# PSUM in four tiles of two banks, and the whole first k tile on the sync queue, in a windowed matmul

## The chip, the cores and the metric

One core of a Trainium2 chip. The metric is device time in microseconds (us) of one execution; most executions agree within 0.3%. The span of a profile runs from its first to its last instruction and is about 1.8 us shorter than the time. TensorE is PE, VectorE is DVE, ScalarE is ACT, GpSimd is POOL and SyncE is SP in the profile.

## The reference

```python
# x [4, 4096, 4096] f32, w [4096, 4096] f32, offsets [4] int64
for b in range(4):
    o = int(offsets[b])
    out[b] = x[b, o:o+64] @ w          # out [4, 64, 4096] f32
```

All of w has to be read (67.1 MB), with 4 x 64 rows of x (4.2 MB), and 4.2 MB have to be written.

## The kernel before

The 256 rows are two groups g of 128. The rows of x are loaded, cast to fp16 and transposed by PE. w is streamed by the POOL queue in blocks of up to four k tiles (a k tile is 128 rows of w), cast to fp16 on the way, into three rotating buffers. Only k tile 0 comes as fp32 by two hardware queues, half of its columns on each, and is cast by ACT. PE writes its sums to tiles in PSUM. Each partial product of 512 columns fills one of eight tiles of 128x512 fp32, which the program names `bank0` to `bank7` and I call banks; it is then evacuated, that is read out and added to `acc` in SBUF, before the program has PE write to that bank again.

```python
ps = [psum_pool.tile([P, NT], fp32, name=f"bank{t}") for t in range(8)]      # NT = 512
...
nc.sync.dma_start(out=w0_32[:, :NG], in_=w[0:P, :NG])
nc.scalar.dma_start(out=off_t[:], in_=offsets[None, :])
nc.scalar.dma_start(out=w0_32[:, NG:], in_=w[0:P, NG:])
...
def add_out(bank, g, c):
    dst = acc[g][:, c * NT : (c + 1) * NT]
    nc.vector.tensor_add(out=dst, in0=dst, in1=ps[bank][:])

def whole_rows(kts, cols, first):          # a block of k tiles, bank after bank
    for g in range(G):
        for c in cols:
            bank = n_bank % 8; n_bank += 1
            for i, kt in enumerate(kts):
                mm(bank, g, kt, ...)
            add_out(bank, g, c)            # cut: the first block copies instead
...
def columns(ng, kts):                      # half of the columns, all 8 banks at once
    for ki in kts:
        for g in range(G):
            for j in range(n_sub):
                tail_mm(ki, g, ng, j, ki == kts[0], ki == kts[-1])
    for g in range(G):
        for j in range(0, n_sub, 2):       # even banks: VectorE adds, odd banks: ACT copies
            add_out(4 * g + j, g, ng * n_sub + j)
            nc.scalar.copy(out=tmp[2 * g + j // 2][:], in_=ps[4 * g + j + 1][:])
    for g in range(G):
        for j in range(1, n_sub, 2):       # then VectorE adds the copies
            nc.vector.tensor_add(...)

columns(order[1], list(join))              # k tiles 25 to 27, first half of the columns
columns(ng, list(join) + list(range(k_tail, n_k)))     # k tiles 25 to 31, second half
for g in range(G):
    store(nc.gpsimd, g, ng * NG, (ng + 1) * NG)        # 2 x 1 MB: the first stores
# cut: k tiles 28 to 31 of the first half, its adds, and four stores of 0.5 MB on two queues
```

I call the two calls of `columns` the short and the long accumulation.

## Time and profile before

| | before |
|---|---|
| time, median of 3 | 182.00 us (181.90 to 182.02) |
| span, mean granted clock | 180.2 us, 0.900 |
| PE / DVE / ACT busy | 127.2 / 90.6 / 18.3 us |
| HBM read / written | 71.30 / 4.19 MB |
| last wait of PE for w, at 164.42 | 0.77 us |
| first store issued | 166.15 us |

The page gives each engine's busy time and, in 40 slices, its busy share in tenths; a 9 is 90% or more. The chain of waits follows back what released what. A row of the timeline starts with start and length in us, and ends with how long the engine had been idle before it and what ended that. The prediction below shows these lines; here it is enough that the DMA engines are full from 3 us to about three before the end (share 0.98 from 3 to 5 us, 1.02 from 175 to 177.5).

### The profile page before, as it was taken

The numbers are of one execution on the slowest core, as the hardware profiler recorded it, in microseconds if no ns is written. First come the engines' busy times: TensorE is split into PE (matmuls) and PEld (weight loads), VectorE is DVE, ScalarE is ACT, GpSimd is POOL, SyncE is SP. The second block draws the span as 40 slices with busy tenths as digits, with TensorE's granted clock in tenths as the row PEclk, the third lists the DMA queues.
The fourth block names the chain that finished last, engine by engine and source line by source line (L and its number), as shares of the span: only waits on it lengthen the run. The fifth ranks groups of instructions, "written<-read, shape, count | busy, mean of one in ns | idle before, by whom it ended". The sixth has DMA issues, their size and how long they took to land.

```text
span 180.2 us, 1537 instructions
## 1 busy us (share of the span) xinstructions
PE 127.2 (71%) x576; PEld 57.0 (32%) x576; DVE 90.6 (50%) x136; ACT 18.3 (10%) x27; POOL 12.7 (7%) x27
## 2 busy tenths in 40 slices
PE   0000789104999499938996599949999999998900
PEld 0000754001344134403442134414444444443400
DVE  0000678100487347833686147725879966409560
ACT  2412556200000000000000000000000004004000
POOL 4600000000000100010001000020007100001100
PEclk9999999855699979996999569987999999999995
DMA  5999989999998899999989999989999999999995
GB/s 186 316 256 216 276 175 204 236 233 226 233 226 189 175 233 233 235 222 233 196 189 211 233 233 218 229 180 213 224 209 215 195 211 213 216 211 208 372 411 209
DMA packets 4152, 40.98 MB, mean 227 GB/s; under 512 B 434, under 2 KB 434, under 8 KB 2226
## 3 DMA queue, kind: packets, MB, share of 16 engines
q0 software_dynamic: 3280, 36.70, 93.4%
q1 hardware_dynamic: 432, 2.10, 3.2%
q10 hardware_dynamic: 434, 2.10, 2.9%
q8 instruction: 4, 0.07, 0.1%
q14 instruction: 2, 0.02, 0.0%
HBM read 71.30 MB, written 4.19 MB: 419 GB/s over the span
## 4 chain that ended last, share of the span: by engine, by line
DMA 58%; PE 30%; issue 3%; DVE 2%; another core or an unknown queue 1%; POOL 1%; POOLq 1%; DVEq 0%
DMA wc<-in_w_dram 58%; PE bank L150 30%; DVE acc L160 2%; POOL wc L114 1%; POOLq L71 1%; POOL xrow L78 0%; DVEq L259 0%; POOL identity masks.py:197 0%; POOLq L78 0%; POOL w L67 0%; POOLq masks.py:199 0%; POOLq L248 0%
## 5 line engine op out<-in xcount | busy, mean ns | idle before, releaser
L150 PE MATMUL bank<-wc,xT 128*128 128x512 f16 x480 | 115.0, 405 | 24.3 <-DMA wc<-in_w_dram 24.3
L160 DVE TENSOR_TENSOR acc<-acc,bank 128x512 f32<-128x512 f32 x112 | 75.2, 687 | 61.5 <-PE bank L150 60.9
L150 PEld LDWEIGHTS <-xT 128*128 128x128 f16 x512 | 52.1, 103 | 93.8 <-DMA wc<-in_w_dram 27.2
L136 PE MATMUL bank<-identity,xrow 128*128 128x128 f16 x64 | 5.3, 258 | 20.0 <-DMA xrow<-in_x_dram 20.0
L203 ACT COPY tmp<-bank 128x512 f32<-128x512 f32 x8 | 4.1, 599 | 127.5 <-PE bank L150 127.5
L145 DVE CAST xT<-bank 128x512 f16<-128x512 f32 x8 | 5.3, 687 | 21.0 <-PE bank L136 20.9
L95 POOL DMA_DIRECT2D wc<-in_w_dram x8 | 4.3, 540 | 108.1 <-PE bank L150 108.1
L136 PEld LDWEIGHTS <-xrow 128*128 128x128 f16 x64 | 5.0, 124 | 20.1 <-issue 20.1
L150 PE MATMUL bank<-w,xT 128*128 128x512 f16 x32 | 7.1, 379 | 0.0
L175 DVE COPY acc<-bank 128x512 f32<-128x512 f32 x8 | 5.4, 688 | 0.9 <-PE bank L150 0.6
L114 POOL DMA_DIRECT2D wc<-in_w_dram x6 | 3.9, 674 | 17.1 <-PE bank L150 17.1
L147 ACT CAST xT<-bank 128x512 f16<-128x512 f32 x8 | 4.4, 593 | 7.1 <-PE bank L136 7.0
L208 DVE TENSOR_TENSOR acc<-acc,tmp 128x512 f32<-128x512 f32 x8 | 5.0, 682 | 0.0
L177 ACT COPY acc<-bank 128x512 f32<-128x512 f32 x8 | 4.7, 586 | 2.1 <-PE bank L150 1.9
L193 POOL DMA_DIRECT2D out_dram<-acc x2 | 1.1, 538 | 26.6 <-DVE acc L208 26.6
L64 ACT CAST w<-acc 128x2048 f16<-128x2048 f32 x1 | 1.9, 1897 | 4.9 <-DMA acc<-in_w_dram 4.9
L78 POOL DMA_DIRECT2D xrow<-in_x_dram x4 | 2.1, 524 | 2.1 <-issue 2.1
L63 ACT CAST w<-acc 128x2048 f16<-128x2048 f32 x1 | 1.9, 1897 | 2.8 <-DMA acc<-in_w_dram 2.8
L63 ACT ACT_TABLE_LOAD x1 | 1.3, 1283 | 1.8 <-PEq L248 1.8
L67 POOL DMA_DIRECT2D w<-in_w_dram x1 | 0.7, 660 | 0.8 <-POOLq L248 0.8
masks.py:199 POOL TENSOR_SCALAR_AFFINE_SELECT identity<-identity 128x128 f16<-128x128 f16 x1 | 0.3, 290 | 0.1
masks.py:197 POOL MEMSET identity<- 128x128 f16 x1 | 0.2, 224 | 0.0
(4 smaller groups left out, 0.4 us busy)
## 6 DMA issues: line engine op xcount, KB each, us to landing
wc<-in_w_dram POOLq DMA_DIRECT2D x5, 4096.0 KB, 42.1
wc<-in_w_dram POOLq DMA_DIRECT2D x4, 1024.0 KB, 24.6
wc<-in_w_dram POOLq DMA_DIRECT2D x1, 3072.0 KB, 37.1
xrow<-in_x_dram POOLq DMA_DIRECT2D x4, 512.0 KB, 14.5
wc<-in_w_dram POOLq DMA_DIRECT2D x1, 2048.0 KB, 26.6
out_dram<-acc POOLq DMA_DIRECT2D x2, 1024.0 KB, 6.3
acc<-in_w_dram SPq DMA_DIRECT2D x1, 1024.0 KB, 5.1
w<-in_w_dram POOLq DMA_DIRECT2D x1, 1024.0 KB, 12.0
```

The lines of the kernel that those rows point to most:

```text
L63: nc.scalar.copy(out=w_one[0][:, :NG], in_=w0_32[:, :NG])
L95: nc.gpsimd.dma_start(out=t[:, base : base + r * N], in_=w[k0 * P : (k0 + r) * P, :].rearrange("(p r) n -> p (r n)", r=r),)
L114: nc.gpsimd.dma_start(out=t[:, pos : pos + n * wd].rearrange("p (t n) -> p t n", t=n), in_=w[ki * P : (ki + n) * P, ng * NG + c0 : ng * NG ...
L136: nc.tensor.matmul(out=ps[t][:, i * P : (i + 1) * P], lhsT=x_cols(g, 4 * t + i), rhs=identity[:], start=True, stop=True,)
L145: nc.vector.tensor_copy(out=dst, in_=ps[t][:])
L147: nc.scalar.copy(out=dst, in_=ps[t][:])
L150: nc.tensor.matmul(out=ps[bank][:], lhsT=xT[g][:, kt * P : (kt + 1) * P], rhs=rhs, start=start, stop=stop,)
L160: nc.vector.tensor_add(out=dst, in0=dst, in1=ps[bank][:])
L175: nc.vector.tensor_copy(out=acc[g][:, c * NT : (c + 1) * NT], in_=ps[bank][:])
L177: nc.scalar.copy(out=acc[g][:, c * NT : (c + 1) * NT], in_=ps[bank][:])
L203: nc.scalar.copy(out=tmp[2 * g + j // 2][:], in_=ps[4 * g + j + 1][:])
L208: nc.vector.tensor_add(out=dst, in0=dst, in1=tmp[2 * g + j // 2][:])
```

## The change

The intent: half as many evacuations, each over two banks, as one add of 1024 columns should take less than two of 512; and the scalar queue left to the offsets alone, which the loads of x wait for. The diff, cut:

```diff
-    tmp = [acc_pool.tile([P, NT], fp32, name=f"tmp{i}") for i in range(4)]
+    tmp = [acc_pool.tile([P, 2 * NT], fp32, name=f"tmp{i}") for i in range(G)]
-    ps = [psum_pool.tile([P, NT], fp32, name=f"bank{t}") for t in range(8)]
+    pairs = [psum_pool.tile([P, 2 * NT], fp32, name=f"banks{t}") for t in range(4)]
+
+    def banks(b, n=1):
+        return pairs[b // 2][:, b % 2 * NT : (b % 2 + n) * NT]
...
-    nc.scalar.dma_start(out=w0_32[:, NG:], in_=w[0:P, NG:])
+    nc.sync.dma_start(out=w0_32[:, NG:], in_=w[0:P, NG:])
...  (transposes and whole_rows: two banks filled, then one evacuation of 1024 columns)
-    def add_out(bank, g, c):
-        dst = acc[g][:, c * NT : (c + 1) * NT]
-        nc.vector.tensor_add(out=dst, in0=dst, in1=ps[bank][:])
+    def add_out(bank, n, g, c):
+        dst = acc[g][:, c * NT : (c + n) * NT]
+        nc.vector.tensor_add(out=dst, in0=dst, in1=banks(bank, n))
...  (columns)
-            for j in range(0, n_sub, 2):
-                add_out(4 * g + j, g, ng * n_sub + j)
-                nc.scalar.copy(out=tmp[2 * g + j // 2][:], in_=ps[4 * g + j + 1][:])
+            add_out(4 * g, 2, g, ng * n_sub)
+            nc.scalar.copy(out=tmp[g][:], in_=banks(4 * g + 2, 2))
...  (last adds)
-            for j in js:
-                add_out(4 * g + j, g, ng * n_sub + j)
+            add_out(4 * g + js[0], 2, g, ng * n_sub + js[0])
```

More of the change, by code (lines that the diff above doesn't have):

```diff
@@ L133 @@
     for g in range(G):
-        for t in range(8):
-            for i in range(4):
+        for t in range(4):
+            for i in range(8):
                 nc.tensor.matmul(
-                    out=ps[t][:, i * P : (i + 1) * P],
-                    lhsT=x_cols(g, 4 * t + i),
+                    out=pairs[t][:, i * P : (i + 1) * P],
+                    lhsT=x_cols(g, 8 * t + i),
                     rhs=identity[:],
@@ L142 @@
                 )
-            dst = xT[g][:, t * NT : (t + 1) * NT]
+            dst = xT[g][:, 2 * t * NT : 2 * (t + 1) * NT]
             if t % 2 == 0:
-                nc.vector.tensor_copy(out=dst, in_=ps[t][:])
+                nc.vector.tensor_copy(out=dst, in_=pairs[t][:])
             else:
-                nc.scalar.copy(out=dst, in_=ps[t][:])
+                nc.scalar.copy(out=dst, in_=pairs[t][:])
     def mm(bank, g, kt, rhs, start, stop):
         nc.tensor.matmul(
-            out=ps[bank][:],
+            out=banks(bank),
             lhsT=xT[g][:, kt * P : (kt + 1) * P],
@@ L156, in mm, with whole_rows @@
         )
-    def add_out(bank, g, c):
-        dst = acc[g][:, c * NT : (c + 1) * NT]
-        nc.vector.tensor_add(out=dst, in0=dst, in1=ps[bank][:])
-    n_bank = 0
-    def whole_rows(kts, cols, first):
-        nonlocal n_bank
-        for g in range(G):
-            for c in cols:
-                bank = n_bank % 8
-                n_bank += 1
-                for i, kt in enumerate(kts):
-                    mm(bank, g, kt, src[kt](c * NT, (c + 1) * NT), i == 0, i == len(kts) - 1)
+    def add_out(bank, n, g, c):
+        dst = acc[g][:, c * NT : (c + n) * NT]
+        nc.vector.tensor_add(out=dst, in0=dst, in1=banks(bank, n))
+    n_pair = 0
+    def whole_rows(kts, first=False):
+        nonlocal n_pair
+        for g in range(G):
+            for c in range(0, 2 * n_sub, 2):
+                b0 = n_pair % 4 * 2
+                n_pair += 1
+                for j in range(2):
+                    for i, kt in enumerate(kts):
+                        rhs = src[kt]((c + j) * NT, (c + j + 1) * NT)
+                        mm(b0 + j, g, kt, rhs, i == 0, i == len(kts) - 1)
+                dst = acc[g][:, c * NT : (c + 2) * NT]
                 if not first:
-                    add_out(bank, g, c)
-                elif c % 2 == 0:
-                    nc.vector.tensor_copy(out=acc[g][:, c * NT : (c + 1) * NT], in_=ps[bank][:])
-                else:
-                    nc.scalar.copy(out=acc[g][:, c * NT : (c + 1) * NT], in_=ps[bank][:])
-    whole_rows([0, 1], range(8), True)
+                    add_out(b0, 2, g, c)
+                elif c % 4 == 0:
+                    nc.vector.tensor_copy(out=dst, in_=banks(b0, 2))
+                else:
+                    nc.scalar.copy(out=dst, in_=banks(b0, 2))
+    whole_rows([0, 1], True)
     for k0, r in blocks[2:-n_join]:
-        whole_rows(range(k0, k0 + r), range(8), False)
+        whole_rows(range(k0, k0 + r))
     join = range(blocks[-n_join][0], k_tail)
@@ L200, in columns @@
         for g in range(G):
-            for j in range(0, n_sub, 2):
-                add_out(4 * g + j, g, ng * n_sub + j)
-                nc.scalar.copy(out=tmp[2 * g + j // 2][:], in_=ps[4 * g + j + 1][:])
+            add_out(4 * g, 2, g, ng * n_sub)
+            nc.scalar.copy(out=tmp[g][:], in_=banks(4 * g + 2, 2))
         for g in range(G):
-            for j in range(1, n_sub, 2):
-                c = ng * n_sub + j
-                dst = acc[g][:, c * NT : (c + 1) * NT]
-                nc.vector.tensor_add(out=dst, in0=dst, in1=tmp[2 * g + j // 2][:])
+            c = ng * n_sub + 2
+            dst = acc[g][:, c * NT : (c + 2) * NT]
+            nc.vector.tensor_add(out=dst, in0=dst, in1=tmp[g][:])
     columns(order[1], list(join))
```

## The prediction

> **What bounds the kernel now.** I read the page first (busy shares, then the 40 slices), then the chain that ended last, the stretches, and last the timeline of the end. The page:
>
> ```profile
> PE 127.2 (71%) x576; PEld 57.0 (32%) x576; DVE 90.6 (50%) x136; ACT 18.3 (10%) x27; POOL 12.7 (7%) x27
> ...
> PE   0000789104999499938996599949999999998900
> ...
> DMA  5999989999998899999989999989999999999995
> ...
> HBM read 71.30 MB, written 4.19 MB: 419 GB/s over the span
> ```
>
> No compute engine is full over the span, but the DMA row is: apart from the first and the last slice it stands at 8 or 9 all the way. PE (the row above) starts at slice 5, has holes until slice 27, and has none from there to the end. The chain of waits, in order of time, says the same (columns: start, length, what):
>
> ```profile
> 6.86 36.20 DMA wc<-in_w_dram
> ...
> 78.28 42.11 DMA wc<-in_w_dram
> 120.39 0.05 issue
> 120.43 15.60 PE bank L150 x64
> ...
> 137.72 26.65 DMA wc<-in_w_dram
> 164.38 0.04 issue
> 164.42 5.37 PE bank L150 x24
> 169.79 1.57 DVE acc L160 x3
> 171.36 0.19 issue
> 171.55 0.69 DVEq L259
> 172.24 1.79 DVE acc L160 x3
> ```
>
> Loads of w stand behind most pieces. The stretches (columns: stretch, length, PE, PEld, DVE, ACT, POOL busy, clock, DMA share, GB/s) show when the load stream ends and what follows:
>
> ```profile
> 120.00:130.00 10.00, 9.57 (x37) 4.03 (x38) 5.50 (x8) 0.00 (x0) 0.00 (x0) 0.83 1.03 221
> 140.00:150.00 10.00, 10.00 (x48) 4.56 (x47) 7.11 (x11) 0.00 (x0) 0.24 (x1) 1.00 0.97 203
> 168.00:170.00 2.00, 2.00 (x11) 0.88 (x9) 0.84 (x2) 0.00 (x0) 0.00 (x0) 1.00 1.06 419
> 174.00:176.00 2.00, 0.00 (x0) 0.00 (x0) 0.04 (x1) 0.00 (x0) 0.00 (x0) 0.73 1.01 412
> ```
>
> The rate doubles at 167.5 us: until then it is casting loads (fp32 read, fp16 written and counted), after that fp32 stores. The DMA share stays near 1.00 through both, until about 177.5. This gives a whole account of the span: about 1.6 us until the first bytes move; 71.30 MB read between there and 167.5, which is 430 GB/s; 4.19 MB of stores at 412 GB/s, 10.2 us, to 177.7; and 2.5 us of last packets, completion and closing. Together 180.2, the span of the page. The 182.0 of the timing is 1.8 more, outside the span.
>
> The last view, the timeline near the end, gives the one place where another engine is close to the path:
>
> ```profile
> 164.42 7.08 PE L150 MATMUL bank<-wc,xT 128*128 128x512 f16 x32 [0.77 <-DMA wc<-in_w_dram]
> 164.57 2.49 DVE L208 TENSOR_TENSOR acc<-acc,tmp 128x512 f32<-128x512 f32 x4
> 166.15 0.54 POOL L193 DMA_DIRECT2D out_dram<-acc  x1 [25.91 <-DVE acc L208]
> 167.35 0.53 POOL L193 DMA_DIRECT2D out_dram<-acc  x1 [0.66 <-DVE acc L208]
> 169.16 4.87 DVE L160 TENSOR_TENSOR acc<-acc,bank 128x512 f32<-128x512 f32 x8 [2.10 <-PE bank L150]
> ```
>
> From 120.43 PE runs 192 matmuls in 43.22 us (the timeline's row for them), 225 ns each with the slow clock at their start, and then waits only 0.77 us for the load at 164.38. So after 120 us PE has 0.77 us to spare and no more. That is the number by which a new PSUM wait has to be judged.
>
> [...] A line through the trace's own two points gives about 1.03 us for 1024.[...] the two halves of the first k tile, 1 MB each on two queues, took 5.1 and 11.3 us to land beside the POOL queue's loads, and the DMA share was full from 3 us on.[...] the change guards by pairs of banks[...] but a bank is now given back only with its neighbour.
>
> **The change part by part.**
>
> *Wide evacuations.* The program's order on VectorE falls from 138 rows to 70: 120 adds and 16 copies of 512 columns become 60 and 8 of 1024. Each pair costs 2 x 0.687 = 1.37 us before[...].[...] the eight adds at the end start every 0.60 us, 0.085 before the one ahead has ended, so a pair costs 1.20 before[...]. ACT: 24 narrow copies become 12 wide ones, 24 x 0.59 = 14.2 us becomes 12 x 1.03 = 12.4. While the load stream is the limit (to 164 us) VectorE waits for PE anyway: 60.9 us in the waits. None of it is on the path there. Matmuls, their number and their order within a bank are the same.
>
> *The end.* With one bank per add, the first of the last eight begins at 169.16, when bank 0 is done. The wide one must wait for bank 1, one matmul later: 0.22 us, so 169.38.[...] The later start eats the saved overhead: 0.0. The first stores of the end, after the adds from tmp, come out the same way: pair 0 at 162.39,[...] Up to 0.2 us earlier, but the DMA engines are still busy with loads until 167.5, so at most 0.1 us.
>
> *PSUM given back later.* At about 150 us one accumulation by columns ends and the next starts with no load wait between. Bank 0 done at T=150.09;[...] PE wants bank 4 again at about T+1.5+0.9=T+2.4. That is 0.2 us of wait which was not there before, and perhaps 0.1 more where the three-tile block before it ends[...]. 0.3 us is inside the 0.77.
>
> *The first k tile on one queue.* The scalar queue loses an issue of 0.38 us; the sync queue issues the second half at about 1.25 instead of 1.41. The first half is no longer in competition with the second, the second follows it[...]. The bytes are the same and the engines were full. So casts of w (5.94 and 12.70) and x rows (18.35) move by a microsecond or so either way, but PE then idles 10.9 us until 43.10 for the next load. On the end: 0.0, with 0.2 either way for the ramp of the first 3 us, where the share was 0.40 and 0.77.
>
> Sum: 0.0 + up to -0.1 + 0.0 + (0.0 plus or minus 0.2), about -0.1 us on 182.0: 181.9.
>
> **The rivals.** First, VectorE sets the pace[...]. For it: 50% busy, and it is on the chain at the end. Against: its waits are for PE, and the stretches have DMA at 1.00 wherever VectorE has its work. Were it so, 175 to 178. Second, four units of PSUM instead of eight stall PE in the stretch without slack. For it: PE is solid from 120.43 to 163.65.[...] If my stall is three times too small, 0.9 against 0.77, the end moves 0.1 to 0.3 us: 182.2; several such stalls, 183. Third, the start: one hardware queue for 2 MB may ramp slower, or x rows come sooner and the stream runs smoother. A shift of the whole stream goes one to one into the end, since it is never idle later: 181.4 to 182.6. Fourth, the clock: the 64-matmul blocks took 15.6 or 16.7 us according to when the slow phase ended; 1.1 us at 120 us would use up the slack and cost 0.3.
>
> **Range and chances.** Four small terms, none over 0.6 us, around 181.9; the three runs before spread by 0.12. I take 181.2 to 182.6. Two per cent is 3.6 us; for a gain of that the load stream would have to lose bytes or gain speed, which nothing in the change does, and for a loss PE would have to stall five times its slack. Faster 0.02, within 0.96, slower 0.02.
>
> **What would show it.** Right:[...] the last load of w landing within 0.5 us of 164.4, DMA full until about 177.5, the last add ending near 174.0, HBM bytes equal. Wrong: a PE wait on VectorE of over 0.8 us between 120 and 164; wide adds over 1374 ns, so that two banks cost extra; the whole stream moved at its start (the load at 43.06 moved by as much as the end); or stores whose rate is not near 412 GB/s.

The sum came to about -0.1 us, 181.9: its terms 0.0 and up to -0.1 (the end), 0.0 (PSUM, as 0.3 us is inside the 0.77) and 0.0 plus or minus 0.2 (the queue); the first three are estimates, as is the first rival's 175 to 178. For the 0.3 the trace of before has a check: there four adds of 512 columns out of PSUM take 2.48 us (from 150.09), so two pairs begun at T+0.22 are done at T+2.70, 0.3 after T+2.4. The 1.03 us for 1024 columns is an estimate for ACT, from its 586 to 599 ns for 512 columns and 1897 for 2048 in that trace.

## The result, and the profile after

| | before | after |
|---|---|---|
| time, median of 6 runs each | 182.01 us (181.86 to 182.07) | 181.99 us (181.76 to 182.03) |
| span, clock | 180.2 us, 0.900 | 180.1 us, 0.900 |
| DVE / ACT busy | 90.6 / 18.3 us | 82.2 / 16.9 us |
| first store issued | 166.15 us | 166.84 us |

The ratio is 0.9998, with a 95% interval of 0.9985 to 1.0011. Ratios here are the mean time of one kernel's fast runs over that of the other's fast runs of the same rounds, so not quite the ratio of the medians quoted; the profiled run is left out of them. The time is the same.

The page of the changed kernel, lines that answer to those shown of before:

```profile
PE 128.2 (71%) x576; PEld 57.3 (32%) x576; DVE 82.2 (46%) x68; ACT 16.9 (9%) x15; POOL 12.7 (7%) x27
...
DMA  5999979999998899999989999999999999999996
...
HBM read 71.30 MB, written 4.19 MB: 419 GB/s over the span
```

VectorE has half of its instructions and 8.4 us less work. The DMA row and the bytes are what they were. The adds as a group, first in the page of before, then in that of after (busy us, mean ns of one, then idle time before them):

```profile
L160 DVE TENSOR_TENSOR acc<-acc,bank 128x512 f32<-128x512 f32 x112 | 75.2, 687 | 61.5 <-PE bank L150 60.9
```

```profile
L164 DVE TENSOR_TENSOR acc<-acc,banks 128x1024 f32<-128x1024 f32 x56 | 67.9, 1221 | 69.0 <-PE banks L154 68.4
```

Busy plus idle is 136.7 us before and 136.9 after. What VectorE saved, 7.3 us in this group, it now waits for PE, 7.5 us more. The chain of waits of the changed kernel in the stretch after 120 us:

```profile
120.44 27.28 PE banks L154 x118
147.72 0.02 issue
147.74 2.76 PE banks L154 x12
150.50 0.02 issue
150.53 0.04 DVE acc L164
150.56 1.10 issue
151.67 1.23 DVE acc L164
152.89 0.04 issue
152.93 10.10 PE banks L154 x46
```

Before, one unbroken piece of PE was followed by a DMA piece. Now DVE pieces stand between pieces of PE: PE waits for PSUM. How long is best read from the starts of the matmuls in the trace. At a granted clock of 1.00, which both traces show from 124 us to the last matmul, they follow each other every 216 ns; I list every larger gap after 124 us, with the number of the matmul since the first streamed tile, counted from 0, and what exceeds 216 ns (single gaps of 10 ns just after one are left out):

```
before   448 at 164.42 us: 935 ns
after    374 at 147.74: 181   392 at 151.80: 181   396 at 152.93: 269
         448 at 164.38: 224   452 at 165.46: 212
```

Matmul 374 is the first of the short accumulation into pair 3, the last pair of the block before it. 392 is the first of the long accumulation, into pair 0; 396 goes into pair 2; 448 and 452 are the same places at the end of the long one (448 also waits for its load, as before). So the single wait of 0.94 us for a load became five of 1.07 us in all, mostly for PSUM. The last matmul starts at 171.29 instead of 171.12.

The timeline of the end, after:

```profile
163.06 2.35 DVE L164 TENSOR_TENSOR acc<-acc,banks 128x1024 f32<-128x1024 f32 x2 [7.91 <-PE banks L154]
...
165.33 2.35 DVE L213 TENSOR_TENSOR acc<-acc,tmp 128x1024 f32<-128x1024 f32 x2
...
166.84 0.54 POOL L200 DMA_DIRECT2D out_dram<-acc  x1 [26.56 <-DVE acc L213]
167.98 0.53 POOL L200 DMA_DIRECT2D out_dram<-acc  x1 [0.59 <-DVE acc L213]
169.55 4.62 DVE L164 TENSOR_TENSOR acc<-acc,banks 128x1024 f32<-128x1024 f32 x4 [1.86 <-PE banks L154]
```

The first store is issued 0.69 us later than before, and the span is still no longer. That is the question for the experiments: what reserve took it up, and how much of it is left?

### The profile page after: what moved, and what is told of

Same layout as the page of the kernel before. It is cut to its first block, busy times and chain, and to the rows that moved or that the text cites. A ratio compares the mean times of both kernels' runs of the same rounds, so it can differ in the third digit from the quotient of the medians.

```text
span 180.1 us, 1403 instructions
## 1 busy us (share of the span) xinstructions
PE 128.2 (71%) x576; PEld 57.3 (32%) x576; DVE 82.2 (46%) x68; ACT 16.9 (9%) x15; POOL 12.7 (7%) x27
## 4 chain that ended last, share of the span: by engine, by line
DMA 43%; PE 43%; issue 4%; DVE 2%; another core or an unknown queue 1%; POOLq 1%; DVEq 1%; POOL 1%
DMA wc<-in_w_dram 43%; PE banks L154 43%; DVE acc L164 2%; DVEq L263 1%; POOLq L75 1%; POOL xrow L82 0%; POOL identity masks.py:197 0%; POOLq L82 0%; POOL w L71 0%; POOLq masks.py:199 0%; DVEq L164 0%; POOLq L252 0%
## 5 line engine op out<-in xcount | busy, mean ns | idle before, releaser
L154 PE MATMUL banks<-wc,xT 128*128 128x512 f16 x480 | 115.8, 405 | 23.6 <-DMA wc<-in_w_dram 23.3
L164 DVE TENSOR_TENSOR acc<-acc,banks 128x1024 f32<-128x1024 f32 x56 | 67.9, 1221 | 69.0 <-PE banks L154 68.4
L140 PE MATMUL banks<-identity,xrow 128*128 128x128 f16 x64 | 5.3, 261 | 19.9 <-DMA xrow<-in_x_dram 19.9
L209 ACT COPY tmp<-banks 128x1024 f32<-128x1024 f32 x4 | 3.9, 1016 | 128.2 <-PE banks L154 128.2
L149 DVE CAST xT<-banks 128x1024 f16<-128x1024 f32 x4 | 4.8, 1222 | 21.5 <-PE banks L140 21.5
L154 PE MATMUL banks<-w,xT 128*128 128x512 f16 x32 | 7.1, 379 | 0.0
L182 DVE COPY acc<-banks 128x1024 f32<-128x1024 f32 x4 | 4.9, 1225 | 1.6 <-PE banks L154 1.6
L213 DVE TENSOR_TENSOR acc<-acc,tmp 128x1024 f32<-128x1024 f32 x4 | 4.7, 1218 | 0.0
L151 ACT CAST xT<-banks 128x1024 f16<-128x1024 f32 x4 | 4.0, 1014 | 7.9 <-PE banks L140 7.9
L184 ACT COPY acc<-banks 128x1024 f32<-128x1024 f32 x4 | 4.0, 1012 | 3.0 <-PE banks L154 3.0
```

The costliest lines, as they stand in the source:

```text
L140: nc.tensor.matmul(out=pairs[t][:, i * P : (i + 1) * P], lhsT=x_cols(g, 8 * t + i), rhs=identity[:], start=True, stop=True,)
L149: nc.vector.tensor_copy(out=dst, in_=pairs[t][:])
L151: nc.scalar.copy(out=dst, in_=pairs[t][:])
L154: nc.tensor.matmul(out=banks(bank), lhsT=xT[g][:, kt * P : (kt + 1) * P], rhs=rhs, start=start, stop=stop,)
L164: nc.vector.tensor_add(out=dst, in0=dst, in1=banks(bank, n))
L182: nc.vector.tensor_copy(out=dst, in_=banks(b0, 2))
```

## The experiments

Twelve kernels, in three batches on three chips, each beside the kernel before. All results are correct but that of the kernel that is wrong. The table has the profiled run's first store and span, then the timed runs.

| run | first store | span | span minus store | time, median | ratio to before (95%) |
|---|---|---|---|---|---|
| before | 166.15 | 180.2 | 14.05 | 182.01 | |
| after | 166.84 | 180.1 | 13.3 | 181.99 | 0.9998 (0.9985-1.0011) |
| e1_queue_only | 166.31 | 180.2 | 13.9 | 181.96 | 0.9993 (0.9979-1.0007) |
| e2_wide_only | 166.83 | 180.0 | 13.2 | 181.98 | 1.0001 (0.9987-1.0014) |
| e3_join_by_bank | 169.26 | 182.1 | 12.8 | 183.76 | 1.0086 (1.0073-1.0100) |
| e4_quads | 168.49 | 182.7 | 14.2 | 184.93 | 1.0164 (1.0137-1.0192) |
| e5_before_dup | 168.10 | 181.0 | 12.9 | 183.19 | 1.0073 (1.0051-1.0095) |
| e6_after_dup | 167.93 | 180.8 | 12.9 | 183.03 | 1.0056 (1.0043-1.0068) |
| e7_one_tile_less | 163.22 | 176.0 | 12.8 | 177.23 | 0.9734 (0.9720-0.9748) |
| e8_vector_extra | 166.97 | 180.2 | 13.2 | 182.02 | 0.9998 (0.9986-1.0011) |
| e9_after_store_late | 168.05 | 180.8 | 12.75 | 183.09 | 1.0061 (1.0031-1.0090) |
| e10_before_store_late | 167.74 | 180.6 | 12.9 | 182.34 | 1.0017 (0.9997-1.0038) |
| e11_store_first | 166.30 | 180.3 | 14.0 | 182.24 | 1.0007 (0.9995-1.0020) |
| e12_act_first | 168.30 | 181.1 | 12.8 | 182.56 | 1.0030 (1.0002-1.0057) |

The theory at first, as in the prediction: the load stream and the stores set the time; VectorE's savings lie beside it; PE has 0.77 us to spare after 120 us, which the later return of PSUM uses up. Rivals: the two parts of the change cancel; VectorE or PE sets the pace.

### The two parts alone

The kernel before with the queue changed:

```diff
-    nc.scalar.dma_start(out=w0_32[:, NG:], in_=w[0:P, NG:])
+    nc.sync.dma_start(out=w0_32[:, NG:], in_=w[0:P, NG:])
```

> The kernel before with only the second half of the first k tile moved from the scalar to the sync queue. Theory (DMA engines shared and full, bytes unchanged): the issue of the second half near 1.3 us instead of 1.41, its landing within 0.3 us of before, the load after the start at 43.0 to 43.1, time within 0.2 us of before. Rival (the two parts of the change cancel, the queue gives a gain or a loss of its own): 0.5 us or more to one side, and the wide kernel alone as much to the other.

The changed kernel with the queue as before:

```diff
-    nc.sync.dma_start(out=w0_32[:, NG:], in_=w[0:P, NG:])
+    nc.scalar.dma_start(out=w0_32[:, NG:], in_=w[0:P, NG:])
```

> The changed kernel with the second half of the first k tile back on the scalar queue, so wide PSUM tiles alone. Theory (VectorE and ACT savings lie beside the load stream, the later return of PSUM is just absorbed by the 0.77 us that PE had to spare): time within 0.2 us of before, PE end near 171.7 as in the changed kernel, VectorE busy near 82. Rival (parts cancel): 0.5 us or more away from before, opposite to the queue alone.

Both came out as the theory says, within 0.1% of before. With the queue alone, the second half was issued at 1.30 us. The cast that waits for the first half began at 5.81 us instead of 5.94, and the cast of the second half at 12.95 instead of 12.70 (12.53 in the changed kernel). Once the slow clock at 120 us had ended, at 124.7 and 125.1 us, PE had in the queue kernel one gap, of 750 ns at 164.39, and in the wide kernel the same five places as after. So the parts do not cancel: each is worth nothing by itself, and the PSUM waits belong to the wide tiles alone.

### What bounds: bytes or VectorE

One k tile not loaded (wrong), in the changed kernel:

```diff
+        rl = r - 1 if k0 == 6 else r
         nc.gpsimd.dma_start(
-            out=t[:, base : base + r * N],
-            in_=w[k0 * P : (k0 + r) * P, :].rearrange("(p r) n -> p (r n)", r=r),
+            out=t[:, base : base + rl * N],
+            in_=w[k0 * P : (k0 + rl) * P, :].rearrange("(p r) n -> p (r n)", r=rl),
         )
         for q in range(r):
-            src[k0 + q] = lambda a, e, t=t, c=base + q * N: t[:, c + a : c + e]
+            src[k0 + q] = lambda a, e, t=t, c=base + min(q, rl - 1) * N: t[:, c + a : c + e]
```

> The changed kernel, wrong on purpose: one k tile of w (2.10 MB of fp32) is not loaded, its neighbour is used twice; every matmul and every evacuation stays. Theory (71.30 MB at 430 GB/s set the time): 2.10 MB / 430 GB/s = 4.9 us less, 177.1. Rival (PE or evacuation sets the pace): less than 2 us less.

The time fell to 177.23 us, 4.8 less, against 4.9 expected, with 576 matmuls and 68 VectorE instructions as in the changed kernel:

```profile
HBM read 69.21 MB, written 4.19 MB: 417 GB/s over the span
```

Extra VectorE work before 120 us, in the changed kernel:

```diff
                 if not first:
                     add_out(b0, 2, g, c)
+                    if kts[0] < 18:
+                        nc.vector.tensor_copy(out=scratch[:], in_=banks(b0))
```

> The changed kernel with an extra VectorE copy of 128x512 out of PSUM after each of the 32 wide adds of the first four blocks (before 120 us): about 32 x 0.65 = 20 us more of VectorE, 82 to 102 us, more than the 90.6 of the kernel before. Theory (VectorE waits for PE there and PE for loads): time within 0.2 us of the changed kernel. Rival (VectorE busy time is worth something, the saved 8 us are a gain hidden by another loss): up by 1 us or more.

Its 0.65 us for a copy is an estimate; in the trace of before the eight copies of this size (L175) take 688 ns each.

```profile
PE 126.6 (70%) x576; PEld 56.8 (32%) x576; DVE 99.0 (55%) x100; ACT 16.9 (9%) x15; POOL 12.7 (7%) x27
```

16.8 us more of VectorE than in the changed kernel, 0.53 a copy (20 were expected), and 182.02 us in the medians of this kernel and of before. VectorE time before 120 us is free in either direction. The two runs together show the first half of the theory: bytes count one for one, evacuation work beside the stream does not.

### What the wide tiles cost: four banks in a tile

The changed kernel again, with two tiles of four banks:

```diff
-    pairs = [psum_pool.tile([P, 2 * NT], fp32, name=f"banks{t}") for t in range(4)]
+    quads = [psum_pool.tile([P, 4 * NT], fp32, name=f"banks{t}") for t in range(2)]
...  (whole_rows, transposes: 2048 columns at once)
-            add_out(4 * g, 2, g, ng * n_sub)
-            nc.scalar.copy(out=tmp[g][:], in_=banks(4 * g + 2, 2))
...
+        add_out(0, 4, 0, c)
+        nc.scalar.copy(out=tmp[:], in_=banks(4, 4))
```

> The changed kernel with two PSUM tiles of four banks and evacuations of 2048 columns (the last adds stay 1024 wide). [...] Theory (what the wide tiles cost is PE waiting for PSUM where it has no load wait to hide it, after 120 us): PE waits about 1.4 us where the three-tile block goes over to columns, and 1.3 us at each of the two ends of a column accumulation, 2.7 to 3.9 us in all; PE ends near 174.5 and the time rises by 1 to 3 us, 183 to 185, with VectorE busy lower still, near 78. Rival (only the load stream counts): within 0.3 us of before.

A straight line through the two measured, 687 ns at 512 columns and 1221 at 1024, gives 2.29 us as an estimate; the adds in the trace of e4 take 2.29.

Its timeline, the places where PE waits:

```profile
148.50 4.48 PE L154 MATMUL banks<-wc,xT 128*128 128x512 f16 x20 [1.51 <-DVE acc L164]
...
154.49 12.25 PE L154 MATMUL banks<-wc,xT 128*128 128x512 f16 x56 [1.51 <-DVE acc L164]
...
168.25 5.34 PE L154 MATMUL banks<-wc,xT 128*128 128x512 f16 x24 [1.52 <-DVE acc L164]
```

Three waits of 1.5 us stand where the theory has them; there are two more, of 0.9 and 0.5 us, in the last eight matmuls. PE ended at 177.06, later than the 174.5 expected, as these two were not in the forecast. The time rose by 2.8 us, within the 1 to 3 expected. Fewer and larger PSUM tiles do cost here, once the waits exceed the reserve: waits for PSUM between 124 and 163 us delay the matmuls by 0 with tiles of one bank (before), 0.63 us with two (after) and 3.36 us with four. The changed kernel is the same thing at a size that still fits.

### A repair that failed: the short accumulation bank by bank

```diff
-        for ki in kts:
-            for g in range(G):
-                for j in range(n_sub):
-                    tail_mm(ki, g, ng, j, ki == kts[0], ki == kts[-1])
+        if ng == order[1]:
+            todo = [(ki, g, j) for g in range(G) for j in range(n_sub) for ki in kts]
+        else:
+            todo = [(ki, g, j) for ki in kts for g in range(G) for j in range(n_sub)]
+        for ki, g, j in todo:
+            tail_mm(ki, g, ng, j, ki == kts[0], ki == kts[-1])
```

> The changed kernel with the matmuls of the first accumulation by columns (25 to 27, all landed) ordered bank by bank, k innermost, so that pairs are completed one after the other and are evacuated before the next accumulation wants them. Theory (the changed kernel's 0.67 us of PE delay by 163 us comes from waits for pairs at the two ends of that accumulation): the first VectorE add after the long accumulation comes at 162.4 to 162.7 instead of 163.06, the wait of PE for the load at 164.4 is back with 0.4 to 0.7 us, the first store is issued 0.3 to 0.6 us earlier than 166.84; the time falls by 0 to 0.3 us only, as the DMA engines are full of loads until 167.5. Rival (the delay comes from elsewhere, e.g. matmul pace): 163.06 stays.

This missed: 1.7 us slower. The expectation says of tiles 25 to 27 that all had landed, and that was wrong:

```profile
149.74 24.35 PE L154 MATMUL banks<-wc,xT 128*128 128x512 f16 x110 [1.39 <-DMA wc<-in_w_dram]
```

k tile 27 has landed at 149.69. With k outermost PE has 16 matmuls of tiles 25 and 26 to do until then (3.5 us); bank by bank it needs tile 27 at the third matmul. The waits at 147.7 and 151.8 are indeed gone from this trace, but for a longer one for a load. It shows how close PE runs behind the loads in this stretch.

### How much reserve: eight matmuls more

In both kernels, each first matmul of the long accumulation is done twice (with start and stop set):

```diff
+                    if ng == order[0] and ki == kts[0]:
+                        tail_mm(ki, g, ng, j, True, True)
                     tail_mm(ki, g, ng, j, ki == kts[0], ki == kts[-1])
```

> The kernel before with eight matmuls more, 128x512, at the start of the long accumulation by columns near 152 us (each done twice, the result is the same): 8 x 0.216 = 1.73 us of PE work. Theory (PE has 0.77 us to spare there): PE ends near 172.5, 1.0 us later, the first store is issued up to 1.7 us later than 166.15 and the DMA engines run empty between the last load at 167.5 and it; time up by 0.8 to 1.4 us. Rival 1 (no slack, PE sets the end): up by 1.7. Rival 2 (the load stream alone sets it): 0.

> The changed kernel with the same eight matmuls more. Theory (the change used up PE's 0.77 us): PE ends 1.73 us later than its 171.67, time up by 1.4 to 1.9 us, that is 0.3 to 0.8 us more than the same addition costs the kernel before. Rival (slack still there): the same rise as in the kernel before.

Rival 2 of the first (0) does not hold: the time rose by 1.3 us (0.9 to 1.7; the medians by 1.2). Rival 1 (1.7) lies at the edge of that interval, but in the trace PE ended at 172.50, 1.0 us later than before and not 1.7, as the theory has it. But the comparison missed: the changed kernel was not hit harder, 1.0 us (0.8 to 1.2), with overlapping intervals. Its profiled run cannot decide it, for a reason worth seeing:

```profile
120.45 13.99 PE L154 MATMUL banks<-wc,xT 128*128 128x512 f16 x64 [3.62 <-DMA wc<-in_w_dram]
...
134.91 14.16 PE L154 MATMUL banks<-wc,xT 128*128 128x512 f16 x64 [0.48 <-DMA wc<-in_w_dram]
```

In this run the block at 120.45 had no slow clock at its start. PE ran its 64 matmuls in 13.99 us, against 15.35 to 16.89 in the other traces, and then waited for loads. Where the slow clock falls changes from run to run: it ended at 123.8 us in the changed kernel, at 124.7 and 125.1 in e1 and e2.

What the pair did give was a better theory. In the runs e3, e5, e6 and e7 the span minus the first store's issue is 12.80 to 12.86 us (the texts below take 12.87), whatever PE did after it; in before and e1 it is about 14, and the span does not fall below 180.0. So: **the stores are an unbroken run of DMA work that begins with the first store, but not before the loads have left the engines.** Below a first store of about 180.1 - 12.87 = 167.2 us nothing is to be gained, and above it each microsecond counts. The reserve is then not PE's 0.77 us but the distance of the first store from 167.2: 1.1 us before and 0.4 us after.

### The first two stores moved, and nothing else

The two stores exchanged, so that the first one waits for the later result, in the changed kernel and in the kernel before (the second then follows it at once, so it moves too, from 167.98 to 168.58 in the changed kernel):

```diff
-    for g in range(G):
+    for g in reversed(range(G)):
         store(nc.gpsimd, g, ng * NG, (ng + 1) * NG)
```

> The changed kernel with the two stores of the first half of the columns in the other order: the POOL queue waits for the later result first, so its first store is issued at about 167.98 instead of 166.84; PE, VectorE and the bytes are as before. New theory (the end is the start of an unbroken run of stores plus a constant: first store issue + 12.87 in the runs where it came late, and no earlier than 180.1, since loads keep the DMA engines until then; so the changed kernel has about 0.4 us to spare there and the kernel before 1.1): span 180.8 to 180.9, time 182.6 to 182.8, up by 0.5 to 0.8 us. Rival (the end follows PE's last matmul and the last adds): no change, 182.0.

> The same exchange of the two stores in the kernel before: first store at about 167.35 instead of 166.15. New theory: 167.35 + 12.87 = 180.2, so 0 to 0.2 us more than before: its 1.1 us to spare take up nearly all of the 1.2 us. Rival (any delay of the first store costs): 1.2 us more. Rival (PE's end counts): no change, which this run alone does not tell from the theory; the one beside it does.

PE and VectorE ran as before it: the last adds of e9 begin at 169.62 (169.55 in the changed kernel) and take 4.62 us. The DMA engines in the stretch 168 to 169, first in the kernel before, then in the changed kernel, then in e9 (the last two columns are DMA share and GB/s):

```profile
168.00:169.00 1.00, 1.00 (x7) 0.43 (x5) 0.00 (x0) 0.00 (x0) 0.00 (x0) 1.00 1.03 379
```

```profile
168.00:169.00 1.00, 1.00 (x6) 0.47 (x5) 0.00 (x0) 0.00 (x0) 0.51 (x1) 1.00 1.10 414
```

```profile
168.00:169.00 1.00, 1.00 (x7) 0.41 (x6) 0.00 (x0) 0.00 (x0) 0.95 (x2) 1.00 0.22 41
```

In e9 the engines run empty for most of a microsecond between loads and stores. In the changed kernel the hand-over is already at its limit: its share from 167.5 to 168 is 0.79, against 1.10 before. The span of e9 grew by 0.6 us (180.15 to 180.79), and the timed runs by 0.6% (1.1 us; 0.6 to 1.6), where the rival says 0. In the kernel before the exchange cost 0.17% (0.3 us, an interval that includes 0): its first store came at 167.74, not the 167.35 expected, as a load landed later in that run; 167.74 + 12.87 is 180.6, and 180.6 is the span. So e9 rules out that only PE and the adds count (against the kernel before; the changed kernel itself was not in this batch), and e10 (at most 0.7 us more) that any delay of the first store costs, as the rival's 1.2 us has it. In the means the exchange costs the changed kernel 0.8 us more than the kernel before, as it must if the change had used the reserve; but the two intervals touch (1.0031 to 1.0090 and 0.9997 to 1.0038), so that difference alone is not clear of noise. The mean of e9 is above the expected 0.5 to 0.8 us. Its six times fall in two groups, 182.2 to 182.6 and 183.6 to 184.0. I return to that below.

### The first store early, PE late

```diff
+        add_out(0, 2, 0, c)
+        nc.scalar.copy(out=tmp[0][:], in_=banks(2, 2))
+        nc.scalar.copy(out=tmp[1][:], in_=banks(4, 2))
+        if ng == order[0]:
+            add_tmp(0, c + 2)              # finish group 0 first
+        add_out(6, 2, 1, c + 2)
...  (then what is left)
```

> The changed kernel with the VectorE order after the long accumulation turned so that the first half-row group is finished first (ACT copies the third pair too): first store issued about 1 us earlier, 165.8, but the fourth PSUM pair is given back about 1 us later, so PE waits, ends at about 172.5 instead of 171.67, and the last add ends at about 175. New theory (first store no later than 167.2, nothing else counts while the last store still finds the engines busy): time within 0.2 us of the changed kernel. Rival (PE's end and the last adds set the end): up by 0.7 to 1.0 us.

```profile
166.30 0.54 POOL L200 DMA_DIRECT2D out_dram<-acc  x1 [25.77 <-DVE acc L209]
...
167.19 5.77 PE L154 MATMUL banks<-wc,xT 128*128 128x512 f16 x26 [0.89 <-DVE acc L164]
```

The first store came 0.5 us earlier, not 1. PE waits 0.9 us more and starts its last matmul at 172.58, 1.3 us later than in the changed kernel; the last add ends at 175.5 instead of 174.2. The time is 182.24 us, 1.0007 of before. So the end of PE and of the adds does not set the time while the last store still finds a queue of others before it. In e4, where the adds ended at 179.0, it did: there the span minus the first store is 14.2, because the stores ran dry in between (DMA share 0.72 from 175 to 176 us and 0.30 from 178 to 179).

### A better order at the hand-over?

```diff
-            add_out(4 * g, 2, g, ng * n_sub)
-            nc.scalar.copy(out=tmp[g][:], in_=banks(4 * g + 2, 2))
+            nc.scalar.copy(out=tmp[g][:], in_=banks(4 * g, 2))
+            add_out(4 * g + 2, 2, g, ng * n_sub + 2)
...  (the adds of tmp move to the first two banks)
```

> The changed kernel with the roles at the ends of the column accumulations exchanged: ACT, the faster one, copies pairs 0 and 2, VectorE adds pairs 1 and 3, so pairs come back at about 1.25, 1.9, 2.2 and 3.0 us after the first bank is done, when PE wants them at 1.7, 2.2, 2.6 and 3.0. Expected: the VectorE work after the long accumulation starts 0.4 to 0.5 us earlier than in the changed kernel, counted from the same bank, the wait of PE for the load at 164.4 comes back with 0.2 to 0.6 us, first store near 166.3 to 166.5. Time within 0.2 us of both kernels, since the floor of the load stream is at 180.1; a version that beats both is not expected from here. Rival (PE delay is what costs): 0.4 us faster than both.

A miss in its mechanism. ACT is the faster one (1016 ns a copy of 1024 columns in the changed kernel, 1221 an add of VectorE), but the waits did not go; they moved to the pairs that VectorE serves. The gaps beyond 216 ns are 181 ns at pair 1 and 268 ns at pair 3, and from the first evacuation after the short accumulation to that after the long one it is 12.53 us in both kernels:

```profile
151.56 1.93 ACT L208 COPY tmp<-banks 128x1024 f32<-128x1024 f32 x2 [116.54 <-PE banks L154]
...
164.09 1.93 ACT L208 COPY tmp<-banks 128x1024 f32<-128x1024 f32 x2 [10.60 <-PE banks L154]
```

Its median is 182.56. Whether the order itself costs anything is not shown: the six times are three of 182.1 to 182.2 and three of 182.9 to 183.5. The profiled run was one of the long ones; the clock granted to PE in it was half until 125.8 us instead of 123.8, and its first store came at 168.30. No version that beats both kernels came out of this.

**Open.** Where the first store is near or past 167.2, single executions were over a microsecond longer in some kernels (e5, e9, e12, one each of e4 and e10), though not in e3 and e6; where it is early they were not (e11 on the same chip as e9 and e12: at most 182.51; the kernel before: at most 182.39 in 31 runs). It fits a slow clock stretch of different length at 120 us, which the reserve of the early ones absorbs. Three profiled runs agree: e6, with no slow clock there, was the shortest of its five (182.59; the others 183.00 to 183.19), e7, where the 118 matmuls from 115.76 us took 28.34 us (27.28 for the 118 from 120.44 in the changed kernel; 216 ns each make 25.5), was the longest of its four (177.86; the others 177.20 to 177.24), and e12, where it lasted until 125.8, was one of its three long ones. But only profiled runs show when the clock was slow, and the mean clock of the others does not sort the long from the short, so it is a reading and not shown. Whether the changed kernel has more of such executions than its six runs (at most 182.03), e8's five (at most 182.10) and e2's five (one of 182.52) let one see is open as well.

## Why the prediction was right, and where its steps were not

*The bound.* Right, and shown by e7: taking 2.1 MB away took 4.8 us away. The prediction's account of the span shows nothing by itself: its two rates and its remainder of 2.5 us are read from the same trace, so they had to add up.

*VectorE and ACT savings worth nothing.* Right (e8). The size of VectorE's saving was 8.4 us, 90.6 to 82.2. The forecast summed durations of adds that overlap in full, 0.687 each, while busy time counts the overlap once (75.2 / 112 = 0.671). The wide add itself took 1221 ns.

*The last adds.* They took 4.62 us, against 4.87 for the eight narrow ones before. They began 0.17 us later than forecast, at 169.55, since PE was that much later.

*PSUM given back later.* Mechanism right, size wrong by a factor of two: 0.3 us forecast before 163 us, 0.63 measured (181 + 181 + 269 ns). The step that failed is "PE wants bank 4 again at about T+1.5+0.9=T+2.4". It took the end of one matmul for the earliest start of the next. By the profile a matmul here is 379 ns long and the next starts 216 ns after it started, 0.16 us before its end. Bank 0 was wanted at T+1.31 (T is now 150.31: the first wide add starts at 150.53, one matmul later) and came back at T+1.44. So even pair 0, for which no wait was forecast, made PE wait, and restarting took another 0.05 us. Pairs 0 and 2 came back at T+1.44 and T+2.57.

*The stores.* "Up to 0.2 us earlier" was wrong in sign: 0.69 us later. The forecast compared the end of an add with the issue of a store (166.15); from the one to the other it takes 0.3 us in both traces. And the first wide add after the long accumulation began at 163.06, not at the 162.39 of the forecast. Without that delay of 0.67 us the store would have been issued at 166.17 (an estimate from these and 166.84), so no gain was there even without the PE waits, and these added the rest.

*The reserve.* The prediction judged the new waits by PE's 0.77 us before the load at 164.38. That the waits before 163 us, 0.63, stay below that figure is no proof: the runs show that this is not what protects the end: in e11 PE ended 1.3 us later at no cost, and in e9 nothing but the first two stores moved, at a cost. By the profiled runs the reserve was 1.1 us at the first store, and the change spent 0.7 of it. That it was enough was luck as far as the prediction goes: it did not know this reserve, and it had put the first store at least 0.7 us too early.

*The queue.* Right, 0.0 (e1). The prediction's 1.25 us for the second issue was 1.30. Its reason does not hold: the two halves were not in competition before either. I added up the DMA packets of the traces by queue. From 3 to 5 us the sync queue, with the first half, had 0.98 to 0.99 of the engines' time and the scalar queue at most 0.03. From 6 to 12 us the POOL queue had 0.68 to 0.73 and the queue with the second half 0.30 to 0.34, in the kernel before as in the changed one.

## What to carry to other kernels

Before you save time on an engine, ask what waits for it last: here 8 us of VectorE became 8 us of waiting for PE. A larger PSUM tile can save evacuation time, here 1221 ns instead of 2 x 687, but is given back later and as a whole, which here cost PE 0.63 us; look for places where one accumulation over all banks follows another, and count from matmul start to matmul start. In a kernel bound by transfers, read the reserve where one stream of transfers hands over to the next, since a change that times the same may have spent it.
